# Regrouping the operand preparation of a decoder layer at the end of its output projection, its FFN gate product and its tail

## The chip, the cores and the metric

The kernel runs on one core of a Trainium2 chip. The core has a matrix engine (TensorE; PE in the profile, with PEld for its weight loads), a vector engine (VectorE, DVE), a scalar engine (ScalarE, ACT), GpSimd (POOL) and SyncE (SP), which only issues DMA transfers here. Each engine works through its own list of instructions in order, and a list waits where an operand is not there yet. The metric is device time in microseconds (us) for one execution; 1256.14 us is the median of three runs before the change.

## The reference

One decoder layer for 1024 prompt tokens and 8 sample tokens, model width 1024. A projection w_in feeds a sliding-window attention and a retention (a linear recurrence in chunks of 128 tokens); both results, side by side, go through w_out; then follow a layer norm with a modulated residual, a SwiGLU FFN of width 2816, and a second layer norm. The shift, scale and gate of each residual come from a small product of `c` with w_ada. Cut to what matters here:

```
def ada_mod(c, w_ada, b_ada):
    m = jax.nn.silu(c) @ w_ada + b_ada
    shift, scale, gate = jnp.split(m, 3, axis=-1)
    return shift[:, None, :], scale[:, None, :], gate[:, None, :]

def swiglu(h, w_up, w_down):
    g, u = jnp.split(h @ w_up, 2, axis=-1)
    return (jax.nn.silu(g) * u) @ w_down

def reference(...):
        mp, kp, vp, sp = mixer_prompt(yp * (1.0 + scp) + shp, ...)     # ends with concat([att, ret]) @ w_out
        ms, ks, vs, ss = mixer_sample(ys * (1.0 + scs) + shs, ...)
        yp = layer_norm(DEEPNORM_ALPHA * yp + (1.0 + gtp) * mp, ln1_w[l], ln1_b[l])
        ys = layer_norm(DEEPNORM_ALPHA * ys + (1.0 + gts) * ms, ln1_w[l], ln1_b[l])
        shp, scp, gtp = ada_mod(c_prompt, w_ada_ffn[l], b_ada_ffn[l])
        shs, scs, gts = ada_mod(c_sample, w_ada_ffn[l], b_ada_ffn[l])
        fp = swiglu(yp * (1.0 + scp) + shp, w_up[l], w_down[l])
        fs = swiglu(ys * (1.0 + scs) + shs, w_up[l], w_down[l])
        yp = layer_norm(DEEPNORM_ALPHA * yp + (1.0 + gtp) * fp, ln2_w[l], ln2_b[l])
```

## The kernel before

**Products.** Every large product is made of three matmuls (`mm3`, L215 to L217): the operands are float32, each is split into a high part (`h`, cast on ACT: L269 for w_in and w_out, L1347 in `split` for the FFN) and a low part (`l`, the difference on DVE: L281 and L1348), and h·h, l·h and h·l are added in PSUM. A weight's life is therefore: DMA into a `raw` (or `wr`) page, cast to `wh` on ACT, difference `wl` on DVE, then matmuls. One split of a 128x1024 page is one ACT and one DVE instruction. The FFN's products use a seven-product scheme, so its operands also need sums and differences of blocks (`up_sums`, L1366 to L1369, and `f_end` and `wd_sums`, L1480 to L1483 and L1513 to L1516) before they are split.

**What sets the order.** The program is written as Python generators. `Merge` runs a main generator (`in_group`, `out_proj`, `ffn`) and fills side streams in between: each stream yields the time that its piece is worth on PE and how long to wait, or a `need` that another stream marks as done. DVE, ACT and POOL run in the order that results from this; so the order in each engine's list is fixed when the program is built. Data pages come from one pool (`page`), so a load can be held by a page that is still in use.

**The stages in time.** The input projection (`pin`) with attention and the samples' retention `samp_ret` runs to 413 us; then `out_proj(0)`, which is the first 512 tokens, and `out_proj(1)`, together `pout`, with the retention chunks in between, to 544; then the FFN's first matrices (`up`, to 1027), then the down projection and the second layer norm (`dn`, to the end).

**Around the end of out_proj(1).** w_out has two column groups, `cg` 0 and 1, of four K-pairs `kp` each (`raw`, `wh`, `wl` of one unit). `w_get` fetches ahead by `depth`: how many units are loaded, cast and differenced in advance, [2, 1, 0] in half 0 and [4, 4, 3] in half 1. Column group 1 of half 1 is done tile by tile: all K for tile 0, then for tiles 1 to 3 (pout of four numbers on PE; m_0 to m_3 are the four pages of the mixed activations). The samples' share is `poutz`, gathered by `samp_sum` (L405 to L408: one copy and three adds into `otz`). Then, per tile, the gated residual (`otmp`, `xr`: L1117, L1118; `xrs` for the samples, L1126), the layer norm's statistics (L1217 to L1236) and the normalisation on ACT (L1238). The samples' `xrs` is transposed in `ln1_s` (`h2ps`, L1264), the prompt's `xr` in `h2_group(1)` (`h2p`, L1292). `h2_group` also makes the FFN's right-hand operands: `hb`, `ts`, `hs_0` to `hs_3`, `hc`. The weights of FFN matrix i are `wa`, `wb`, `wc`, `wd`, from two loads `wr`, prepared by `up_prep`.

**Other places the change touches.** `ada_gate_a` and `ada_gate_b` make the second gate (`which == 2`) from w_ada_ffn: loads `adr`, matmuls `adab` (L878) and `gsels` (L902), as a side stream during the input projection and `out_proj(0)`. In `samp_ret` (L949 on), the four state pages `st` and the four broadcasts `vb` are all loaded first. `f_end` and `wd_sums` for the last pair run right after the last `up`. `z_affine` (L1629) scales a 128x1024 page of the residual. `KM` is where the last column group of `dn` stops being done for all four tiles at a time: 11 K-steps, of which those from KM on are done tile by tile, three matmuls each.

Of the kernel before, what the change touches and what calls it, by code (L numbers as in the profile page):

```python
# [23 lines left out]
NP = NF // 2  # L24
# [13 lines left out]
KM = 4  # L38
# [139 lines left out]
def emit(ctx, tc, I, O):  # L178
# [644 lines left out]
    def ret_M(c):  # L823
# [4 lines left out]
        half, tl = c // 4, c % 4  # L828
        for j in range(2):
            mh, ml = mix_pages(half, 2 + j)  # L830
            oh = mh[:, 0:1024].rearrange("p (a c) -> p a c", a=2)[:, :, tl * 128:(tl + 1) * 128]
            ol = ml[:, 0:1024].rearrange("p (a c) -> p a c", a=2)[:, :, tl * 128:(tl + 1) * 128]
            for a in range(2):
                h = 2 * j + a
                src, g = b[:, h * 128:(h + 1) * 128], gnT[:, h:h + 1]
                A.mul(oh[:, a], src, g)
                V.scalar_tensor_tensor(out=ol[:, a], in0=src, scalar=g, in1=f(oh[:, a]), op0=ALU.mult,
                                       op1=ALU.subtract)
# [110 lines left out]
    def samp_ret():  # L949
# [5 lines left out]
        state_pg = []  # L955
        for i in range(4):
# [3 lines left out]
            state_pg.append(t)  # L960
# [3 lines left out]
        vb = []  # L964
        for i in range(4):
            t = page(f"vb{i}")
            SP.dma_start(out=t[:, 0:1024], in_=vd[2 * i:2 * i + 2, :].rearrange("(o b) e -> o (b e)", o=1)
                         .to_broadcast([128, 1024]))
            vb.append(t)
        yield 0, 4000, 3000  # L970
        b = bank("srt")
# [14 lines left out]
        for i in range(4):  # L986
            st = state_pg[i]
# [15 lines left out]
            yield 430, 0  # L1003
# [124 lines left out]
    def out_proj(half, with_s):  # L1128
        yield ("need", ("att", half))
        if half == 1:  # L1130
            depth[:] = [4, 4, 3]
        for cg in range(2):
# [334 lines left out]
    def f_end(P):  # L1467
# [16 lines left out]
        for p, ap in ((1, a11), (2, a12), (4, a22)):  # L1484
            d = drp.tile([128, 512], F32, name=f"fd{p}_{P}")
            G.dma_start(out=two(d) if p == 4 else d, in_=ap)  # L1486
            FD[p, P] = d
# [172 lines left out]
    def ffn():  # L1660
# [15 lines left out]
        f_end(NP - 1)  # L1676
        wd_sums(NP - 1)
# [135 lines left out]
    if True:  # L1813
# [20 lines left out]
        M.add([ada_gate_a(1), ada_gate_a(2)])  # L1834
# [61 lines left out]
```

## Time and profile before

| | value |
|---|---|
| time of the runs shown | 1257.42, 1256.14, 1255.63 us |
| the profiled execution: its time, its span | 1258.56 us, 1256.8 us |
| TensorE, busy | 1213.2 us, 97% of the span; 43.6 us not busy |
| VectorE, busy | 875.0 us, 70% |
| ScalarE, busy | 469.6 us, 37% |
| GpSimd, busy | 93.9 us, 7% |
| mean granted TensorE clock | 0.98 of full speed |
| w_up loads | 44 of 512 KB, 5.2 us each from issue to landing |

TensorE is the engine that is nearly always busy, so the profile is read for the places where it is not: what its instructions wait for (the view of waits), how busy each engine was in a stretch and at which clock (the view of windows), and the instructions one by one (the timeline). In a timeline row stand the start, the duration, the engine, the line and the operation, what goes in and out, how many alike were put together (x), and in brackets how long the engine had been idle before and which instruction ended that.

### The profile page before, as it was taken

What the parts mean: (1) busy time and instruction counts of PE and PEld (TensorE: products, weight loads), DVE (VectorE), ACT (ScalarE), POOL (GpSimd) and SP (SyncE); (2) the same over time, 40 slices, a digit from 0 to 9 for tenths busy, and PEclk for the clock granted to TensorE, in tenths of its full rate; (3) what the DMA queues carried; (4) which work ended last, traced back from release to release, by engine and by line L of the source; (5) the groups of instructions that cost most, each with busy time, mean ns of one, the idle gap of its engine ahead of it and who ended that gap; (6) DMA issues with size and microseconds to landing.
All of it is one profiled execution on the core that took longest, in us unless ns stands there. A gap on an engine that the chain in (4) does not pass through costs nothing.

```text
span 1256.8 us, 20184 instructions
## 1 busy us (share of the span) xinstructions
PE 1213.2 (97%) x7923; PEld 1023.8 (81%) x7923; DVE 875.0 (70%) x1749; ACT 469.6 (37%) x876; POOL 93.9 (7%) x130
## 2 busy tenths in 40 slices
PE   8999989999999999987999999999999999999996
PEld 5877756788877677677999999999999987888885
DVE  3456665787654687877767676667666769849697
ACT  2345543355543335545232322232223234434420
POOL 0000000001000002020110111011101110000011
PEclk8999999999999999997999999999999999999998
DMA  9732387242226432412443444344434499746631
GB/s 290 230 118 68 125 271 258 68 153 87 68 68 217 147 124 79 149 69 68 147 165 109 163 156 159 110 156 156 159 110 167 144 362 389 264 152 218 201 119 67
DMA packets 143999, 198.81 MB, mean 158 GB/s; under 512 B 8127, under 2 KB 85163, under 8 KB 143888
## 3 DMA queue, kind: packets, MB, share of 16 engines
q1 hardware_dynamic: 133376, 161.11, 39.6%
q0 software_dynamic: 10528, 36.42, 7.5%
q8 instruction: 62, 1.02, 0.3%
q14 instruction: 33, 0.27, 0.1%
HBM read 154.76 MB, written 43.77 MB: 158 GB/s over the span
## 4 chain that ended last, share of the span: by engine, by line
PE 54%; issue 29%; DVE 9%; POOL 4%; DMA 2%; ACT 1%; POOLq 0%; SPq 0%; DVEq 0%
PE pin L215 6%; PE pin L216 6%; PE pin L217 6%; PE dn L216 4%; PE dn L217 4%; PE dn L215 4%; PE up L215 2%; PE up L217 2%; PE up L216 2%; PE adab L878 2%; PE pout L215 1%; POOL fd L1486 1%; PE pv L671 1%; PE sps L628 1%; PE pout L216 1%
## 5 line engine op out<-in xcount | busy, mean ns | idle before, releaser
L215 PE MATMUL pin<-wh,hT 128*128 128x512 f32 (+1 forms) x320 | 129.6, 410 | 1.8 <-ACT qk L781 1.6
L216 PE MATMUL pin<-wl,hT 128*128 128x512 f32 (+1 forms) x320 | 124.8, 390 | 3.3 <-DVE wl L281 3.3
L217 PE MATMUL pin<-wh,hT 128*128 128x512 f32 (+1 forms) x320 | 124.3, 390 | 0.0
L215 PE MATMUL up<-hb,wa_h 128*128 128x256 f32 (+1 forms) x352 | 100.3, 286 | 6.9 <-ACT wa_h L1347 3.3
L216 PE MATMUL up<-hb,wa_h 128*128 128x256 f32 (+1 forms) x352 | 100.4, 285 | 0.4 <-DVE hb L1308 0.4
L217 PE MATMUL up<-hb,wa_l 128*128 128x256 f32 (+1 forms) x352 | 100.1, 285 | 0.2 <-DVE wa_l L1348 0.2
L215 PEld LDWEIGHTS pin<-wh,hT 128*128 128x128 f32 x320 | 61.1, 192 | 31.0 <-issue 13.9
L281 DVE TENSOR_TENSOR wl<-raw,wh 128x1024 fp32r<-128x1024 f32 (+1 forms) x62 | 73.1, 1183 | 7.3 <-ACT wh L269 3.6
L215 PEld LDWEIGHTS up<-hb,wa_h 128*128 128x128 f32 x352 | 67.3, 192 | 7.6 <-ACT wa_h L1347 3.5
L216 PEld LDWEIGHTS pin<-wl,hT 128*128 128x128 f32 x320 | 61.5, 192 | 14.4 <-DVE wl L281 3.4
L217 PEld LDWEIGHTS pin<-wh,hT 128*128 128x128 f32 x320 | 61.2, 191 | 14.0 <-issue 0.8
L1453 ACT ACTIVATE sg<-sg 128x256 f32<-128x256 f32 (+1 forms) x63 | 26.4, 420 | 115.3 <-DVE sg L1452 115.3
L216 PEld LDWEIGHTS up<-hb,wa_h 128*128 128x128 f32 x352 | 67.6, 192 | 0.6 <-DVE hb L1308 0.6
L217 PEld LDWEIGHTS up<-hb,wa_l 128*128 128x128 f32 x352 | 67.4, 192 | 0.4 <-DVE wa_l L1348 0.4
L269 ACT CAST wh<-raw 128x1024 fp32r<-128x1024 f32 (+1 forms) x62 | 62.9, 1020 | 6.8 <-DMA raw<-in_w_in 6.3
L1472 ACT COPY hTs<-sg 128x8 f32<-128x8 f32 x22 | 4.3, 198 | 138.9 <-DVE sg L1459 138.9
L1458 DVE TENSOR_TENSOR uc<-up,tp 128x256 f32<-128x256 f32 x66 | 28.2, 427 | 39.0 <-PE up L217 38.9
L1452 DVE TENSOR_TENSOR sg<-up,tp 128x256 f32<-128x256 f32 (+1 forms) x63 | 26.7, 423 | 38.2 <-PE up L217 38.2
L216 PE MATMUL pout<-wl,mh 128*128 128x512 f32 x128 | 50.8, 397 | 2.5 <-DVE wl L281 2.5
L215 PE MATMUL pout<-wh,mh 128*128 128x512 f32 x128 | 51.1, 408 | 0.0
L217 PE MATMUL pout<-wh,ml 128*128 128x512 f32 x128 | 51.0, 398 | 0.0
L215 PE MATMUL up<-hc,wc_h 128*128 128x256 f32 (+1 forms) x176 | 49.9, 284 | 0.0
(508 smaller groups left out, 3624.4 us busy)
## 6 DMA issues: line engine op xcount, KB each, us to landing
wr<-in_w_up SPq DMA_DIRECT2D x44, 512.0 KB, 5.2
raw<-in_w_in SPq DMA_DIRECT2D x38, 512.0 KB, 3.6
adr<-in_w_ada_ffn SPq DMA_DIRECT2D x24, 512.0 KB, 3.9
wd<-in_w_down SPq DMA_DIRECT2D x22, 512.0 KB, 5.2
dr<-fs SPq DMA_DIRECT2D x44, 256.0 KB, 2.8
dr<-ws SPq DMA_DIRECT2D x44, 256.0 KB, 3.7
fd<-sg POOLq DMA_DIRECT2D x33, 256.0 KB, 3.9
dr<-fd SPq DMA_DIRECT2D x33, 256.0 KB, 7.3
```

The lines of the kernel that those rows point to most:

```text
L215: PE.matmul(ps, lhsT=ah, rhs=bh, start=start, stop=False, skip_group_check=onto)
L216: PE.matmul(ps, lhsT=ah, rhs=bl, start=False, stop=False, skip_group_check=onto)
L217: PE.matmul(ps, lhsT=al, rhs=bh, start=False, stop=stop, skip_group_check=onto)
L269: A.copy(out=h[:, 0:n], in_=src[:, 0:n])
L281: V.tensor_sub(out=l[:, 0:n], in0=src[:, 0:n], in1=f(h[:, 0:n]))
L628: PE.matmul(bk[:, i1 * 256:i1 * 256 + n], lhsT=qT[b][:, h * 128:(h + 1) * 128], rhs=kv[:, k0 + off:k0 + 256], start=s == 0, stop=s == 1)
L671: PE.matmul(bk[64 * par:64 * par + 64, 0:256].rearrange("p (a c) -> p a c", a=2), lhsT=v, rhs=pv[:, kt, par::2, :], start=kt == k0, stop=k ...
L878: PE.matmul(b[32 * q:32 * q + 32, :], lhsT=cT[:, k2 * 4 + q, :], rhs=rr[q // 2][:, (q % 2) * 512:(q % 2) * 512 + 512], start=k2 == 0, stop ...
L1452: V.tensor_tensor(out=dst, in0=ps, in1=add, op=ALU.add)
L1453: A.activation(out=dst, in_=dst, func=AF.Silu)
L1458: V.tensor_tensor(out=t, in0=ps, in1=add, op=ALU.add)
L1486: G.dma_start(out=two(d) if p == 4 else d, in_=ap)
```

## The change

It makes eight edits.

- `samp_sum` copies 40 rows on ACT and adds twice on DVE instead of three times.
- `ret_M` issues four ACT multiplications, then four DVE instructions, instead of alternating.
- `samp_ret` loads `st` and `vb` in pairs: the first pair, the second after the ropes, the third and fourth when a pair has been used.
- The second gate (`ada_gate_a(2)`, `ada_gate_b(2)`) is a stream of its own behind the samples' normalised rows ("xns"), so it runs in `out_proj(1)` and the first FFN matrix.
- `depth` is [3, 2, 1] in half 0 and [3, 3, 2] in half 1.
- A new stream `up_first` prepares FFN matrix 0 as soon as the last of w_out has been fetched ("wload") and the sums and `wa` of matrix 1 once tile 7 is done; it ends with a one-column Silu on ACT. `ln1_s` waits for "outs", set right after `out_samp`, no longer for the whole of `out_proj(1)`.
- `f_end` for the last pair is stopped after its stores; its sums and `wd_sums` follow at steps 2 and 4 of the down projection, `samp_z` at 6, and the `z_affine` steps are spread by the list `ZAT`.
- `KM` is 3.

```diff
-KM = 4
+ZAT = [6, 8, 10, 12, 14, 16, 18, 20, 22, 24, 25, 26, 27, 28, 29, 30]
+KM = 3
...
     def samp_sum(dst, b, n):
-        A.copy(out=dst, in_=b[0:8, 0:n])
-        for g in range(1, 4):
-            V.tensor_tensor(out=dst, in0=dst, in1=b[32 * g:32 * g + 8, 0:n], op=ALU.add)
+        t = tmp512("ssum")
+        A.copy(out=t[0:40, 0:n], in_=b[0:40, 0:n])
+        V.tensor_tensor(out=t[0:40, 0:n], in0=t[0:40, 0:n], in1=b[64:104, 0:n], op=ALU.add)
+        V.tensor_tensor(out=dst, in0=t[0:8, 0:n], in1=t[32:40, 0:n], op=ALU.add)
...
+        for oh, ol, src, g in hs:
+            A.mul(oh, src, g)
+        for oh, ol, src, g in hs:
+            V.scalar_tensor_tensor(out=ol, in0=src, scalar=g, in1=f(oh), op0=ALU.mult, op1=ALU.subtract)
...
     def ada_gate_a(which):
+        if which == 2:
+            yield "need", "xns"
...
+        st_load(0)
         rr = page("rrs")
         ropefull(rr[0:8, 0:512], zqgs[:, 0:512], C("src")[0:8], C("srs")[0:8], 8)
         ropefull(rr[0:8, 512:1024], zkvs[:, 0:512], C("src")[32:40], C("srs")[32:40], 8)
...
         yield 0, 4000, 3000
+        st_load(1)
...
+            vb.pop(i)
+            if i < 2:
+                st_load(i + 2)
+            yield 430, 6000
...
     def out_proj(half, with_s):
         yield ("need", ("att", half))
-        if half == 1:
-            depth[:] = [4, 4, 3]
+        depth[:] = [3, 2, 1] if half == 0 else [3, 3, 2]
...
+                if half == 1 and cg == 1 and kp == 0:
+                    done.add("wload")
...
                 out_samp(cg, psz)
+                done.add("outs")
                 for t in range(4):
-                    if t == 1:
-                        up_prep(-AHEAD[1])
-                    if t == 2:
-                        up_prep(-AHEAD[0])
...
+    def up_first():
+        yield "need", "wload"
+        up_prep(-AHEAD[1])
+        yield 0, 4000
+        for n in (-3, -1, 1, 3):
+            up_prep(n)
+            yield 0, 0, 2500
+        yield "need", ("outt", 7)
+        done.add("first")
+        up_prep(0)
+        yield 0, 4000
+        up_prep(4)
+        t = small("silu", [128, 1])
+        A.activation(out=t, in_=identr[:, 0:1].bitcast(F32), func=AF.Silu)
+
     def ln1_s():
-        yield "need", ("out", 1)
+        yield "need", "outs"
...
-            if r[1] == 0 or "ahead" in done:
+            if r[1] == 0 or "ahead" in done or ("first" in done and r[0] <= 7):
...
-        f_end(NP - 1)
-        wd_sums(NP - 1)
+        fe = f_end(NP - 1)
+        next(fe)
+        for e in range(2):
+            r = (2 * (NP - 1) + e) * 128
+            WD[1 + e, NP - 1] = I["w_down"][r:r + 128, 0:512]
...
                 if n == 2:
+                    next(fe, None)
+                if n == 4:
+                    wd_sums(NP - 1)
+                if n == 6:
                     samp_z()
-                if 5 <= n < 21:
-                    z_affine((n - 5) // 2, (n - 5) % 2)
-                elif n == 21:
+                if n in ZAT:
+                    z_affine(ZAT.index(n) // 2, ZAT.index(n) % 2)
+                elif n == 23:
...
-        M.add([ada_gate_a(1), ada_gate_a(2)])
+        M.add([ada_gate_a(1)])
...
-        M.add([ada_gate_b(1), ada_gate_b(2)])
+        M.add([ada_gate_b(1)])
         M.run(out_proj(0, False), R3)
         M.add([ln1_tile(t) for t in range(4)] + [h2_group(0)], 2)
-        M.add([ln1_tile(t) for t in range(4, 8)] + [ln1_s(), h2_group(1)], 2)
+        M.add([up_first()])
+        M.add([ada_gate_a(2), ada_gate_b(2)])
+        M.add([ln1_s()])
+        M.add([ln1_tile(t) for t in range(4, 8)] + [h2_group(1)], 2)
```

How this moves instructions shows at three places. A row gives the line, the operation and out<-in; a number behind a name tells pages of one name apart, and the lines are some ten to thirty higher after the change.

**Place one: DVE in the input projection, around the samples' ropes (`rrs`, `rtmp`), the state updates (`st`) and a w_in difference.** Before:

```order
L719 TENSOR_TENSOR rrs<-rrs,rtmp 8x512 x2
L976 COPY qss<-srt 128x4x8
L977 TENSOR_SCALAR kss<-srt 128x4x8
L994 SCALAR_TENSOR_TENSOR st_1712<-vb_1731,kss,st_1712 128x128 x6
L281 TENSOR_TENSOR wl_1748<-raw_1594,wh_1707 128x1024
```

The same w_in difference, of raw_1594, in the changed kernel's DVE list:

```order
L718 TENSOR_TENSOR rrs<-zsr,cst 8x512
L282 TENSOR_TENSOR wl_1736<-raw_1594,wh_1707 128x1024
L721 TENSOR_TENSOR rrs<-rrs,rtmp 8x512
L718 TENSOR_TENSOR rrs<-zsr,cst 8x512
L721 TENSOR_TENSOR rrs<-rrs,rtmp 8x512
L984 COPY qss<-srt 128x4x8
```

The difference moved ahead of the last ropes and of six state updates.

**Place two: PE at the end of out_proj(1), column group 1.** The four tiles are pout_4998 to pout_5001 before and pout_4945 to pout_4948 after. Before, at the last tile's share of m_1 and what follows it:

```order
L217 MATMUL pout_5001<-wh_4758,ml_1_3257 128x512
L215 MATMUL pout_5001<-wh_4863,mh_2_4277 128x512
L1174 MATMUL poutz<-raw_4941,mixTs 32x512 x2
L216 MATMUL pout_4998<-wl_4945,mh_2_4277 128x512
L217 MATMUL pout_4998<-wh_4863,ml_2_4278 128x512
```

The changed kernel's PE list at the corresponding point, the end of the first three tiles' share of m_0:

```order
L217 MATMUL pout_4947<-wl_4812,mh_0_3133 128x512
L218 MATMUL pout_4947<-wh_4705,ml_0_3134 128x512
L216 MATMUL pout_4947<-wh_4810,mh_1_3187 128x512
L1186 MATMUL poutz<-raw_4888,mixTs 32x512
L217 MATMUL pout_4945<-wl_4892,mh_1_3187 128x512
L218 MATMUL pout_4945<-wh_4810,ml_1_3188 128x512
```

And where its third tile is complete:

```order
L217 MATMUL pout_4947<-wl_4965,mh_3_4236 128x512
L218 MATMUL pout_4947<-wh_4951,ml_3_4237 128x512
L1289 MATMUL h2ps<-cst,xrs 128x8 x8
L216 MATMUL pout_4948<-wh_4705,mh_0_3133 128x512
L217 MATMUL pout_4948<-wl_4812,mh_0_3133 128x512
L218 MATMUL pout_4948<-wh_4705,ml_0_3134 128x512
```

Before the change, the matmuls of m_0 and m_1 for all four tiles stand ahead of the first one that needs the third unit's difference (wl_4945, K-pair 2). After it, the matmuls of m_0 for three tiles stand ahead of the first one that needs the second unit's difference (wl_4892, K-pair 1), and the fourth tile stands behind the transposes of the samples' rows (h2ps), which in the kernel before come after all tiles.

**Place three: DVE at the same point, from the second half's first residuals on.** Before:

```order
L1118 SCALAR_TENSOR_TENSOR xr_3_4937<-xr_3_4937,otmp 128x512
L1126 SCALAR_TENSOR_TENSOR xrs<-xrs,otz 8x512
L281 TENSOR_TENSOR wl_4945<-raw_4861,wh_4863 128x1024
L281 TENSOR_TENSOR wl_5002<-raw_4941,wh_4943 128x1024
L408 TENSOR_TENSOR otz<-otz,poutz 8x512 x3
```

The changed kernel's DVE list, at the first of its differences of column group 1 that stands behind the residuals:

```order
L1137 SCALAR_TENSOR_TENSOR xrs<-xrs,otz 8x512
L1226 BN_STATS lst<-xrs 8x6
L1226 BN_STATS lst<-xr_0_4878 128x6
L282 TENSOR_TENSOR wl_4892<-raw_4808,wh_4810 128x1024
L1226 BN_STATS lst<-xr_1_4880 128x6
L282 TENSOR_TENSOR wl_4953<-raw_4888,wh_4890 128x1024
```

And, a little later, what stands between the samples' gated residual and its norm:

```order
L1137 SCALAR_TENSOR_TENSOR xrs<-xrs,otz 8x512
L1391 TENSOR_TENSOR sb_4985<-wr_1_4960 128x512
L1393 TENSOR_TENSOR sa_4984<-wr_0_4958,wr_1_4960 128x512
L1392 TENSOR_TENSOR sa_4984<-sb_4985,wr_0_4958 128x512
L1128 TENSOR_TENSOR otmp<-pout_4945,gate_4220 128x512
L1394 TENSOR_TENSOR sb_4985<-wr_0_4958,sa_4984 128x512
L1373 TENSOR_TENSOR wa_l<-wr_0_4958,wa_h 128x1024
L1373 TENSOR_TENSOR wb_l<-sa_4984,wb_h 128x1024
L1373 TENSOR_TENSOR wc_l<-sb_4985,wc_h 128x1024
L1414 TENSOR_TENSOR wd_5002<-wr_1_4960,wd_5002 128x512
```

So at this place DVE delivers the second unit's difference where it delivered the third's before, and all of FFN matrix 0's operands (sums sa, sb and differences wa_l, wb_l, wc_l, wd) are made in one piece behind the fourth unit.

More of the change, by code (lines that the diff above doesn't have):

```diff
@@ L828, in ret_M @@
         half, tl = c // 4, c % 4
+        hs = []
         for j in range(2):
@@ L834, in ret_M @@
                 h = 2 * j + a
[L835 to L838, printed above, removed]
+                hs.append((oh[:, a], ol[:, a], b[:, h * 128:(h + 1) * 128], gnT[:, h:h + 1]))
+        for oh, ol, src, g in hs:
+            A.mul(oh, src, g)
+        for oh, ol, src, g in hs:
+            V.scalar_tensor_tensor(out=ol, in0=src, scalar=g, in1=f(oh), op0=ALU.mult, op1=ALU.subtract)
     def ret_chunk(c):
@@ L954, in samp_ret, with st_load @@
         yield "need", ("zs", "rq")
-        state_pg = []
-        for i in range(4):
+        state_pg, vb = {}, {}
+        def st_load(i):
             t = page(f"st{i}")
@@ L959, in samp_ret @@
                          in_=I["state"][8 * i:8 * i + 8].rearrange("a d e -> d a e"))
-            state_pg.append(t)
+            state_pg[i] = t
+            t = page(f"vb{i}")
+            SP.dma_start(out=t[:, 0:1024], in_=vd[2 * i:2 * i + 2, :].rearrange("(o b) e -> o (b e)", o=1)
+                         .to_broadcast([128, 1024]))
+            vb[i] = t
+        st_load(0)
         rr = page("rrs")
@@ L963, in samp_ret @@
         ropefull(rr[0:8, 512:1024], zkvs[:, 0:512], C("src")[32:40], C("srs")[32:40], 8)
[L964 to L969, printed above, removed]
         yield 0, 4000, 3000
+        st_load(1)
         b = bank("srt")
@@ L986, in samp_ret @@
         for i in range(4):
-            st = state_pg[i]
+            st = state_pg.pop(i)
             s4 = st[:, 0:1024].rearrange("p (b h e) -> p b h e", b=2, h=4)
@@ L1002, in samp_ret @@
                         in_=st[:, 0:1024].rearrange("p (a e) -> p a e", a=8))
-            yield 430, 0
+            vb.pop(i)
+            if i < 2:
+                st_load(i + 2)
+            yield 430, 6000
         yield "need", ("zs", "rg")
@@ L1473, in f_end @@
                    in_=t[:, 512:NT].rearrange("p (b c) -> p b c", b=2)[:, :, 256:260])
-        sa, sb = page(f"fsa{P}"), page(f"fsb{P}")
         def two(ap):
             return ap.rearrange("p (b c) -> p b c", b=2)
+        for p, ap in ((1, a11), (2, a12), (4, a22)):
+            d = drp.tile([128, 512], F32, name=f"fd{p}_{P}")
+            G.dma_start(out=two(d) if p == 4 else d, in_=ap)
+            FD[p, P] = d
+        yield
+        sa, sb = page(f"fsa{P}"), page(f"fsb{P}")
         s2, s3, s1, s4 = sa[:, 0:512], sa[:, 512:1024], sb[:, 0:512], sb[:, 512:1024]
@@ L1483, in f_end @@
         V.tensor_sub(out=s4, in0=a12, in1=s2)
[L1484 to L1487, printed above, removed]
         for p2, t in (((6, 7), sa), ((5, 3), sb)):
@@ L1530, in emit @@
         n0 = 14 * (P + 1)
-        side.setdefault(n0, []).append((f_end, P))
+        side.setdefault(n0, []).append((lambda P: list(f_end(P)), P))
         side.setdefault(n0 + 1, []).append((wd_load, P))
```

## The prediction

> **What bounds the kernel now.** I read the busy times first, then what TensorE waits for, then the stretches in which it waits.
>
> ```profile
> span 1256.8 us, 20184 instructions
> PE 1213.2 (97%) x7923; PEld 1023.8 (81%) x7923; DVE 875.0 (70%) x1749; ACT 469.6 (37%) x876; POOL 93.9 (7%) x130
> ```
>
> TensorE is idle for 1256.8 - 1213.2 = 43.6 us; the other engines have room over the whole span. No matmul is removed, so the change can win only idle time, matmuls at a low clock, and the tail behind the last matmul. The view of waits (total us, times, longest) says where the idle time is:
>
> ```profile
> PE pin L216 <- DVE wl L281: 3.3, 1, 3.3
> ...
> PE pout L216 <- DVE wl L281: 2.5, 2, 1.2
> ...
> PE dn L216 <- DVE d_1l L1348: 1.6, 1, 1.6
> ...
> PE dn L216 <- DVE d_0l L1348: 1.1, 1, 1.1
> ...
> PE dn L216 <- DVE d_10l L1348: 0.4, 1, 0.4
> ```
>
> Nearly each row is one hole, and these wait for low parts (`wl`, `d_1l`) that DVE makes late. The windows show busy us of PE, PEld, DVE, ACT and POOL, then the granted clock:
>
> ```profile
> 180.00:190.00 10.00, 7.69 (x43) 5.34 (x44) 10.00 (x39) 0.84 (x2) 0.00 (x0) 0.83 0.79 259
> 390.00:450.00 60.00, 60.00 (x332) 41.73 (x328) 35.71 (x95) 19.57 (x43) 2.61 (x3) 0.97 0.48 167
> 450.00:460.00 10.00, 8.77 (x40) 6.54 (x40) 9.86 (x19) 6.85 (x16) 0.56 (x1) 1.00 0.50 133
> 580.00:590.00 10.00, 5.49 (x31) 4.42 (x31) 8.20 (x15) 5.24 (x10) 0.00 (x0) 0.82 0.39 107
> 590.00:600.00 10.00, 10.00 (x73) 10.00 (x73) 7.06 (x11) 4.22 (x6) 0.00 (x0) 0.84 0.21 61
> 515.90:590.00 74.10, 60.32 (x335) 48.81 (x335) 62.68 (x124) 34.65 (x50) 6.37 (x10) 0.91 0.28 90
> ```
>
> Behind holes the clock is 0.82 to 0.84 over 10 us, so a hole of about 3 us costs its length and (1 - 0.84) x 10 = 1.6 us more. From 390 to 450 TensorE is full, at 450 DVE is.
>
> **Input projection: -4.9 us.** The hole at 180:
>
> ```profile
> 176.34 1.28 DVE L719 TENSOR_TENSOR rrs<-rrs,rtmp 8x512 f32<-8x512 f32 x2
> 179.46 1.67 DVE L994 SCALAR_TENSOR_TENSOR st<-vb,kss,st 128x128 f32<-128x128 f32 x6
> 181.04 1.22 DVE L281 TENSOR_TENSOR wl<-raw,wh 128x1024 fp32r<-128x1024 f32 x1
> 182.31 0.50 PE L216 MATMUL pin<-wl,hT 128*128 128x512 f32 x1 [3.31 <-DVE wl L281]
> ```
>
> The difference waits behind ropes and six state updates. In the new order it stands ahead of the last ropes, near 176, some 5 us earlier, and TensorE needs it at 179. The hole goes (3.3) and the low clock after it (1.6): -4.9. What is late next is the second difference, which now stands behind 8 state updates (1.67 / 6 x 8 = 2.2 us) and has that slack. Bounds: -2 (the hole reappears there) to -5.
>
> By the Trainium skill (TensorE: Matmul & The Clock Gate, "What's actually happening") the half clock follows at least one idle window of about 3.4 us, of a window that runs freely. Here 3.31 us of idle time was enough. By the rule a hole just under the window may cost no clock, and this term would be -3.3; the row says -4.9, which I take.
>
> **The second gate: -5.9 us ahead of out_proj(1).**
>
> ```profile
> 417.38 1.06 PE L878 MATMUL adab<-adr,cT 128*32 128x512 f32 x8
> 441.53 1.03 PE L902 MATMUL gsels<-adg,cst 128*9 128x512 f32 x2
> ```
>
> Of the gate's products, four groups like the first (1.0 us from start to start) and two like the second (0.95) leave a stretch in which TensorE is full, by the window of 390 to 450: 4 x 1.0 + 2 x 0.95 = 5.9. With them go eight loads on SP and the evacuations on ACT. Later they fall into holes (below), where they cost nothing; if those holes close, the 5.9 come back there. At 450 DVE is 99% busy, so part of it may be given back by TensorE arriving early there: bounds 0 to -6. The other edits between 250 and 490 (the shorter `samp_sum`, four ACT multiplications first in `ret_M`, one unit more of fetching in half 0) touch holes of about 5 us and add none that I see: 0, bounds -2.5 to +2.5.
>
> **The end of out_proj(1): +5.5 us.** I count from U = 515.9, where column group 0 ends on TensorE.
>
> ```profile
> 516.00 1.06 PE L1174 MATMUL poutz<-raw,mixTs 128*32 128x512 f32 x8
> 522.71 0.40 PE L216 MATMUL pout<-wl,mh 128*128 128x512 f32 x1
> 522.95 0.40 PE L217 MATMUL pout<-wh,ml 128*128 128x512 f32 x1
> 525.74 1.21 DVE L1348 TENSOR_TENSOR hs_3l<-ts,hs_3h 128x1024 fp32r<-128x1024 f32 x1
> 527.58 0.69 DVE L1117 TENSOR_TENSOR otmp<-pout,gate 128x512 f32<-128x512 f32 x1
> 528.19 0.68 DVE L1217 BATCH_NORM_STATS2 lst<-xr 128x6 f32<-128x512 f32 x1
> 532.62 2.34 DVE L281 TENSOR_TENSOR wl<-raw,wh 128x1024 fp32r<-128x1024 f32 x2
> 533.88 0.50 PE L216 MATMUL pout<-wl,mh 128*128 128x512 f32 x1 [1.23 <-DVE wl L281]
> 543.94 0.40 PE L217 MATMUL pout<-wh,ml 128*128 128x512 f32 x1
> ```
>
> Before, the difference that stops TensorE is the third unit's, at 533.8, and the matmuls of two units in four tiles cover all but 1.23 us. The last pout starts at 543.94: T = U + 28.4.
>
> In the new order DVE does the same up to `hs_3l` (near 526.6), then eleven instructions of 0.61 from start to start (xr four times, otmp, ssum, otz twice, xrs, two statistics), then the difference: 526.6 + 6.7 + 1.2 = 534.5 = U + 18.6. But this is the second unit's, and ahead of it TensorE has only three tiles of the first: 21 matmuls x 0.23 (522.95 - 522.71) and nine `poutz` (the row above is four of them, 1.0 us), 7.1 us, so it runs dry at U + 7.5. **A hole of about 11 us.** Then the first three tiles, 51 matmuls, 12 us, bring it to U + 31.3.
>
> There the samples' transposes `h2ps` need the norm of `xrs`. On DVE it stands behind all of FFN matrix 0's preparation:
>
> ```profile
> 539.67 0.67 DVE L1366 TENSOR_TENSOR sb<-wr 128x512 f32<-128x512 f32 x1
> 543.53 1.25 ACT L1238 ACTIVATE xr<-xr,lrs 128x1024 f32<-128x1024 f32 x1 [9.23 <-DVE lrs L1236]
> 544.62 1.22 DVE L1348 TENSOR_TENSOR wa_l<-wr,wa_h 128x1024 fp32r<-128x1024 f32 x1
> ```
>
> The third and fourth differences and two `otz` and `xrs` end at U + 25; four sums and `wd` (5 x 0.61), three splits (3 x 1.2) and `otmp`, `xr`, statistics and small ones (4.5) give U + 36.6, the norm on ACT U + 38. A second hole of 6.5 us. Transposes, tile 3 (24 matmuls, 5.6 us) and a group of the gate follow: T = U + 45.4, or U + 47 with the low clock behind both holes. Thus T is 17 to 18.6 us later.
>
> What was to be won:
>
> ```profile
> 581.63 1.23 DVE L1348 TENSOR_TENSOR hs_3l<-ts,hs_3h 128x1040 fp32r<-128x1040 f32 x1
> 587.40 0.58 PE L215 MATMUL up<-hb,wa_h 128*128 128x256 f32 x1 [3.26 <-ACT wa_h L1347]
> ```
>
> Before, FFN matrix 1 starts at 587.40, 43.5 us behind T, and runs at half speed until 593; that costs about 2.6, so it effectively starts at 590.0 = U + 74.1. In the new order matrix 0's sums and splits (7 us of DVE) no longer lie between T and `hs_3l`, and matrix 1's sums and `wa` are made ahead of it. Walking the DVE list with the durations above, `hs_3l` ends 31.9 us behind T, and matrix 1 starts 1.3 later without its stall: U + 78.6 to U + 80.2. TensorE's work there, 169 FFN matmuls of 0.12, 32 transposes (3.7) and the rest of the gate (4.9), is 29 us and fits within 33. Difference to U + 74.1: +4.5 to +6; I take **+5.5**. Bounds: between U and 590, DVE is busy 62.7 of 74.1 us by the window, so no order wins more than 11.4; and +9 if the loads of w_out that now stand behind those of `xr` on SP come late as well.
>
> The same section of the Trainium skill speaks against this part: both holes are above its 3.4 us, so by it a cold stretch follows each for certain, which is the U + 80.2 case.
>
> The dummy Silu has no input that binds it to its place: its table load stands at the start of ACT's list, and the load ahead of the first real Silu is still there. It moves nothing: 0.
>
> **Down projection: -3.1 us.**
>
> ```profile
> 1027.40 0.69 DVE L1480 TENSOR_TENSOR fsb<-sg,sg 128x512 f32<-128x512 f32 x1
> 1029.41 1.04 ACT L1347 CAST d_1h<-dr 128x1024 fp32r<-128x1024 f32 x1
> 1032.34 1.22 DVE L1348 TENSOR_TENSOR d_1l<-dr,d_1h 128x1024 fp32r<-128x1024 f32 x1
> 1061.17 1.21 DVE L1629 TENSOR_TENSOR z<-z,ln_wb 128x1024 f32<-128x1024 f32 x1
> ```
>
> Eight sums of 0.61 from 1027.40 on stand ahead of `d_1l` and leave the place. Then ACT's cast bounds it: 1030.4 + 1.2 = 1031.6, and TensorE, which waited 1.6 us up to 1033.6, had matmuls until 1032.0, so that hole goes. By 1061 four of the z instructions (1.2 each) fewer have run on DVE, as `ZAT` spreads them; that covers the holes of 1.1 and 0.4 at `d_0l` and `d_10l`. 1.6 + 1.1 + 0.4 = 3.1. Bounds -1.5 (the eight sums, made some steps later, open the later holes again) to -3.4.
>
> **The tail: -1.5 us.**
>
> ```profile
> 1245.92 0.39 PE L217 MATMUL dn<-d_10h,d_10l 128*128 128x512 f32 x1
> 1242.49 0.69 DVE L1657 TENSOR_TENSOR zt<-dn,gate 128x512 f32<-128x512 f32 x1
> 1247.90 0.68 DVE L1657 TENSOR_TENSOR zt<-dn,gate 128x512 f32<-128x512 f32 x1
> ```
>
> DVE takes 5.4 us per tile (1242.49 to 1247.90), TensorE 21 x 0.232 = 4.9, so DVE falls behind; the last tile's norm starts at 1247.90, 1.6 us behind the end of the last matmul, 1246.31. With KM at 3 a tile takes 24 x 0.232 = 5.6 and DVE follows at once. Bounds 0 to -1.6.
>
> **Sum.** -4.9 - 5.9 + 5.5 - 3.1 - 1.5 = -9.9. Against the profiled execution, 1258.56 (span 1256.8 and 1.8 around it), that is 1248.7; it was 2.4 above the median 1256.14, so I forecast 1246.
>
> **Rivals.**
> - *The holes of out_proj(1) don't open* (the differences come earlier than my walk has them, since `hs` waits less): that term becomes -8 to -11, and the time 1230 to 1233. For it: DVE has 11.5 us of room there; against it: the order of its list is fixed, and eleven instructions stand ahead. 0.12.
> - *The gain ahead of out_proj(1) is eaten*: DVE is 99% busy at 450, so TensorE's 5.9 us become a wait there, and the low clock at 180 stays: -9.9 + 5.9 + 1.6 = -2.4 gives 1253.7. For it: that DVE row; against: from 390 to 450 DVE is busy for only 35.7 of 60 us, so it can work ahead. 0.20.
> - *out_proj(1) loses it all* (slower): one mechanism, the two late differences. If w_out's last two loads, now behind the four of `xr`, land late, the third and fourth difference open holes of their own, and T slips on. From +15.4 instead of +5.5 the sum is zero; at +19 the time is 1259.7. Against: the loads' pages come free with column group 0, 10 us ahead. 0.10.
> - *It doesn't do what it says:* of the preload of the table that holds; it is in the sum at 0.
>
> **How the numbers follow.** Forecast 0.58, the rivals as above. The range leaves out half of the first and nearly all of the slow case: 1232 to 1255. A measurement of this kernel can tell about 0.2% (2.5 us) from no change. Faster by more: the forecast, the first rival and half of the second, 0.80; within: the other half, 0.10; slower: 0.10.
>
> **What would show it.** No 3.3 us wait for `wl` in pin; gate products among `up`, none at 417; a wait of pout for `wl` of some 11 us and one of `h2ps` for ACT of some 6.5; no wait of `up` for `wa_h`; none of `dn` for `d_1l`; the last `zt` at once behind the last matmul. If the two long waits are absent, the first rival holds; if they are much longer, the third.

## The result and the profile after

The changed kernel takes 1262.95 us, the median of five runs (1262.29 to 1266.62), where the kernel before takes 1256.14 beside it: a ratio of 1.006, interval [1.0042, 1.0078]. It is slower by some 7 us, where 10 less were forecast, and lies outside the range. The profiled execution took 1266.6 us, with a span of 1264.8. Its page begins:

```profile
span 1264.8 us, 20175 instructions
PE 1217.7 (96%) x7923; PEld 1020.3 (81%) x7923; DVE 868.2 (69%) x1741; ACT 469.0 (37%) x879; POOL 93.2 (7%) x130
```

The span grew by 8.0 us, TensorE's idle time by only 3.5 (47.1 against 43.6): the other 4.5 is busy time, for the same 7923 matmuls. That is the first hint that this is not a story of waits alone. What TensorE waits for now (us in total, times, longest):

```profile
PE pout L217 <- DVE wl L282: 11.4, 3, 10.2
PE h2ps L1289 <- ACT xrs L1247: 5.8, 1, 5.8
PE up L216 <- DVE tp L1462: 4.4, 4, 2.0
PE rmt L829 <- DVE sm L755: 2.5, 2, 1.7
...
PE dn L217 <- DVE d_0l L1373: 1.1, 1, 1.1
PE dn L217 <- DVE d_8l L1373: 1.0, 1, 1.0
```

The waits of `up` for `wa_h` (3.3) and of `dn` for `d_1l` (1.6) are gone, that of `pin` for `wl` fell from 3.3 to 0.4, and two long ones are new, as forecast. In the timeline:

```profile
528.60 1.20 DVE L282 TENSOR_TENSOR wl<-raw,wh 128x1024 fp32r<-128x1024 f32 x1
529.85 0.80 PE L217 MATMUL pout<-wl,mh 128*128 128x512 f32 x1 [10.21 <-DVE wl L282]
...
532.71 1.93 PE L1186 MATMUL poutz<-raw,mixTs 128*32 128x512 f32 x6
...
535.30 0.69 DVE L409 TENSOR_TENSOR ssum<-ssum,poutz 40x512 f32<-40x512 f32 x1 [3.78 <-ACT ssum L408]
...
551.53 1.01 PE L1289 MATMUL h2ps<-cst,xrs 8*128 8x8 f32 x8 [5.81 <-ACT xrs L1247]
...
562.45 1.07 PE L882 MATMUL adab<-adr,cT 128*32 128x512 f32 x8
```

U (the second piece of `poutz`) now stands at 510.2. The late difference comes at U + 19.6 (forecast 18.6) and opens a hole of 10.21 us (forecast 11). `h2ps` starts at U + 41.3 (forecast 38): behind the hole `poutz` ran at half clock, 1.93 us, and DVE waited 3.78 for it. Its hole is 5.81 (forecast 6.5). The row of `adab` at 562 is the second gate's second group; its first stands at 555, behind both holes.

The windows below cut each profile at 30 us (behind the start, which the change leaves alone), at U, at the start of the first and at the end of the last `dn` matmul. The columns are the stretch, then busy us of PE, PEld, DVE, ACT and POOL, then the granted clock. The kernel before:

```profile
30.00:516.00 486.00, 477.64 (x2878) 362.27 (x2877) 316.50 (x846) 223.44 (x502) 20.49 (x28) 0.99 0.43 140
516.00:1027.30 511.30, 494.94 (x3939) 471.87 (x3938) 363.22 (x665) 157.43 (x276) 54.19 (x82) 0.98 0.44 145
1027.30:1246.30 219.00, 215.65 (x931) 173.08 (x930) 179.79 (x209) 81.86 (x85) 15.95 (x13) 1.00 0.61 214
```

The changed kernel, and below them the stretch from the last `pout` (T) to the start of FFN matrix 1, and two more:

```profile
30.00:510.20 480.20, 473.05 (x2846) 360.35 (x2844) 309.48 (x838) 219.07 (x500) 19.53 (x27) 0.99 0.42 134
510.20:1036.50 526.30, 503.19 (x3973) 470.89 (x3973) 363.36 (x664) 159.75 (x279) 53.99 (x83) 0.98 0.45 148
1036.50:1255.50 219.00, 216.60 (x934) 172.75 (x932) 180.93 (x211) 81.84 (x85) 16.86 (x14) 1.00 0.61 216
560.70:597.10 36.40, 33.55 (x231) 25.35 (x230) 24.41 (x53) 21.25 (x33) 1.51 (x3) 1.00 0.39 133
180.00:190.00 10.00, 10.00 (x65) 5.94 (x64) 6.41 (x27) 3.13 (x6) 0.00 (x0) 1.00 0.72 230
1050.00:1090.00 40.00, 37.99 (x160) 29.29 (x159) 39.94 (x39) 18.07 (x21) 2.74 (x4) 1.00 0.93 342
```

Each stretch is split three ways: *idle* is its length less PE's busy time; *low clock* is the busy time that a clock under 1 cost, the sum over windows of 2 us of busy time x (1 - granted clock); the rest is TensorE's *work*, what it would need at full clock without a wait. In us:

| | before | after | difference | forecast |
|---|---|---|---|---|
| 30 us to U: idle + low clock | 8.4 + 6.8 | 7.1 + 3.3 | -4.8 | -4.9 |
| U to the first `dn`: idle + low clock | 16.4 + 7.3 | 23.1 + 6.8 | +6.2 | +5.5 |
| work, 30 us to U | 470.9 | 469.8 | -1.1 | -5.9 |
| work, U to the first `dn` | 487.7 | 496.4 | +8.7 | 0 |
| first to last `dn` | 219.0 | 219.0 | 0.0 | -3.1 |
| behind the last `dn` | 10.5 | 9.4 | -1.1 | -1.5 |
| sum | | | +7.9 | -9.9 |

The two rows of idle time and low clock came out nearly as forecast, the first of them in part by luck (below). TensorE's work did not: -5.9 was expected, and it is +7.6.

### The profile page after: what moved, and what is told of

Read it like the earlier page. It is cut to its first block, busy times and chain, and to the rows that moved or that the text cites. A ratio compares the mean times of both kernels' runs of the same rounds, so it can differ in the third digit from the quotient of the medians.

```text
span 1264.8 us, 20175 instructions
## 1 busy us (share of the span) xinstructions
PE 1217.7 (96%) x7923; PEld 1020.3 (81%) x7923; DVE 868.2 (69%) x1741; ACT 469.0 (37%) x879; POOL 93.2 (7%) x130
## 4 chain that ended last, share of the span: by engine, by line
PE 42%; issue 28%; DVE 6%; POOL 4%; DMA 3%; ACT 1%; POOLq 0%; DVEq 0%; SPq 0%; ACTq 0%
PE dn L217 4%; PE dn L216 4%; PE dn L218 4%; PE pin L216 3%; PE pin L218 3%; PE pin L217 3%; PE up L216 2%; PE up L217 2%; PE up L218 2%; DMA dr<-fd 2%; PE pout L217 2%; PE pout L218 2%; PE pout L216 1%; POOL fd L1504 1%; POOL fs L1515 1%
## 5 line engine op out<-in xcount | busy, mean ns | idle before, releaser
L216 PE MATMUL pin<-wh,hT 128*128 128x512 f32 (+1 forms) x320 | 128.3, 405 | 0.8 <-ACT hT L340 0.8
L218 PE MATMUL pin<-wh,hT 128*128 128x512 f32 (+1 forms) x320 | 122.9, 384 | 0.0
L217 PE MATMUL up<-hb,wa_h 128*128 128x256 f32 (+1 forms) x352 | 99.1, 282 | 1.1 <-DVE hb L1333 1.1
L216 PE MATMUL up<-hb,wa_h 128*128 128x256 f32 (+1 forms) x352 | 99.0, 282 | 0.0
L217 PE MATMUL pout<-wl,mh 128*128 128x512 f32 x128 | 53.6, 420 | 11.4 <-DVE wl L282 11.4
```

What stands on the lines that cost most here:

```text
L216: PE.matmul(ps, lhsT=ah, rhs=bh, start=start, stop=False, skip_group_check=onto)
L217: PE.matmul(ps, lhsT=ah, rhs=bl, start=False, stop=False, skip_group_check=onto)
L218: PE.matmul(ps, lhsT=al, rhs=bh, start=False, stop=stop, skip_group_check=onto)
```

## The experiments

All in one table: the median of the runs, the ratio to the kernel before with its interval, the number of *packed pieces*, and the three parts of the stretch from 30 us to the first `dn`. A packed piece is an unbroken row, in PE's list, of the 32-column products `adab` and `poutz` (four matmuls make a whole group of `adab`); the number is counted in the programs.

| | time us | ratio | pieces | work | idle | low clock |
|---|---|---|---|---|---|---|
| before | 1256.14 | 1 | 24 | 958.6 | 24.8 | 14.1 |
| after | 1262.95 | 1.0060 [1.0042, 1.0078] | 30 | 966.2 | 30.2 | 10.1 |
| e1_depth | 1261.78 | 1.0043 [1.0024, 1.0062] | 29 | 964.7 | 27.4 | 12.1 |
| e2_first | 1261.76 | 1.0044 [1.0028, 1.0059] | 32 | 968.5 | 25.4 | 7.6 |
| e3_both | 1257.95 | 1.0020 [1.0004, 1.0036] | 31 | 965.7 | 23.5 | 9.0 |
| e4_qorder | 1256.50 | 1.0000 [0.9985, 1.0015] | 22 | 953.8 | 30.9 | 11.1 |
| e5_wlfirst | 1256.81 | 1.0012 [0.9998, 1.0027] | 31 | 966.4 | 22.9 | 6.9 |
| e6_gate_moved | 1249.83 | 0.9946 [0.9926, 0.9967] | 22 | 954.3 | 23.4 | 13.7 |
| e7_gate_back | 1257.38 | 1.0008 [0.9993, 1.0023] | 22 | 958.5 | 27.7 | 8.2 |
| e8_before_qorder | 1255.42 | 0.9996 [0.9973, 1.0019] | 22 | 956.0 | 21.9 | 10.0 |
| e9_lns_back | 1252.00 | 0.9969 [0.9956, 0.9982] | 22 | 955.7 | 23.9 | 11.8 |
| e10_first_kept | 1251.21 | 0.9963 [0.9949, 0.9976] | 23 | 955.8 | 23.9 | 10.2 |
| e11_sums_back | 1247.38, one run | | 22 | 956.7 | 23.5 | 6.7 |
| e12_samples_first | 1248.60 | 0.9945 [0.9926, 0.9964] | 23 | 956.3 | 23.6 | 8.4 |

Single executions of one kernel lie 3 to 6 us on either side of the median, mostly by stretches of low clock that come and go, so the last two columns of one profile are known to some 3 us only. The work is steadier: up to U, where the changed kernel, e1, e2, e3 and e5 have the same pieces, it is 469.3 to 469.9 in their profiles, while low clock is 3.3 to 6.8.

**Depth and stream.** One part undone at a time, then both.

```diff
-        depth[:] = [3, 2, 1] if half == 0 else [3, 3, 2]
+        depth[:] = [3, 2, 1] if half == 0 else [4, 4, 3]
```

> The changed kernel with the fetch-ahead of out_proj(1) set back to [4, 4, 3]; all else as changed. Theory A (two separate late deliveries): the 10.2 us wait of pout for wl goes with the low clock behind it, and the wait of h2ps for the samples' norm stays at about 6 us: some 11 us less than the changed kernel, 1252. Theory B (one chain on VectorE from the end of column group 0 to the samples' norm): the norm comes only earlier by what VectorE idles in that stretch (3.8 us behind poutz, and the second poutz pieces), so the wait moves from wl to h2ps, which grows to 11 to 13 us: some 4 us less, 1259.

1261.78 us. The waits for `wl` fell to 7.9 in total (longest 6.8) and did not go, as both theories had it; that of `h2ps` rose to 7.4, and T moved from U + 50.5 to U + 47.7 only. That is nearer to theory B: half of what is taken from the first hole stands in the second. Theory A (1252) falls, and the old depth alone does not close the first hole.

For the second, `up_first` goes, and `up_prep(-AHEAD[1])` and `up_prep(-AHEAD[0])` stand in the loop over the tiles again.

```diff
-        M.add([up_first()])
```

> The changed kernel without the new stream up_first: FFN matrix 0 prepared between the tiles as before the change; fetch-ahead stays [3, 3, 2]. Theory A: the 10.2 us wait of pout for wl stays, the 5.8 us wait of h2ps goes with its low clock: some 7 us less, 1256. Theory B: VectorE's preparation of matrix 0 (7 us) and the sums of matrix 1 only move behind tile 3 and lengthen the way from there to FFN matrix 1, whose wait for wa_h (3.3 us) comes back: within 2 us of the changed kernel, 1261 to 1265.

1261.76 us. The long wait for `wl` stays (10.2), and the waits of `up` for `wa_h` (2.8) and `wb_h` (1.4) come back, as theory B has it.

> The changed kernel with both undone: fetch-ahead [4, 4, 3] and no up_first. Theory A: both waits go, some 18 us less than the changed kernel, 1245. Theory B: the stretch from the end of column group 0 to FFN matrix 1 goes back to its length before the change (74 us against 87), some 13 us less, 1250.

1257.95 us: both theories were too good. Of its waits:

```profile
PE pout L217 <- DVE wl L282: 7.9, 3, 6.8
...
PE h2ps L1293 <- ACT xrs L1251: 1.3, 1, 1.3
```

With both parts undone the wait for `h2ps` is nearly gone, but a hole of 6.8 for `wl` stays, and the kernel is still not faster than before. Yet its idle time is 1.3 us below that of before and its low clock 5.1 below, while its work is 7.1 above. So the holes are not the whole cause: a part of it lies in TensorE's work.

**Packed pieces.** In the changed kernel many groups of `adab` are cut in two or three by other matmuls, since their four matmuls need two loads (`rr[0]` for q of 0 and 1, `rr[1]` for 2 and 3), of which the second comes later. With the order turned, the group waits for the later load and runs whole.

```diff
-            for q in range(4):
+            for q in (2, 3, 0, 1):
```

> The changed kernel with one edit in ada_block: the four matmuls of a group are issued in the order 2, 3, 0, 1, so that the first of them needs the later of the two loads; the list then has 16 whole groups of adab where the changed kernel has 24 pieces. Theory (a piece of the small products costs about 1.0 us on TensorE whether it holds one, two or four matmuls): five to eight pieces fewer ahead of the end of out_proj(1) and in FFN matrix 0, some 5 us less, 1258. Rival (a piece costs 0.25 us for each matmul in it): no change, 1262 to 1264.

1256.50 us: 6.4 us won against the changed kernel by the order of four matmuls, both holes as long as they were (10.2 and 6.1). What a piece costs is seen in PE's timeline. The changed kernel:

```profile
411.41 0.40 PE L218 MATMUL pout<-wh,ml 128*128 128x512 f32 x1
411.73 1.05 PE L882 MATMUL adab<-adr,cT 128*32 128x512 f32 x2
412.71 0.27 PE L1097 MATMUL spt<-cst,Ps 64*128 64x64 f32 x1
412.91 1.05 PE L882 MATMUL adab<-adr,cT 128*32 128x512 f32 x2
413.89 0.50 PE L216 MATMUL pout<-wh,mh 128*128 128x512 f32 x1
```

The same place with whole groups (e4_qorder):

```profile
408.56 0.40 PE L216 MATMUL pout<-wh,mh 128*128 128x512 f32 x1
408.88 1.06 PE L882 MATMUL adab<-adr,cT 128*32 128x512 f32 x8
409.88 0.50 PE L217 MATMUL pout<-wl,mh 128*128 128x512 f32 x1
410.22 0.39 PE L218 MATMUL pout<-wh,ml 128*128 128x512 f32 x1
```

The trace shows two records for each of these float32 matmuls. A piece of one matmul (x2) lasts 0.98 us from start to start, a piece of four (x8) 1.00. From 408.56 to 410.22 are 1.66 us, where two `pout` matmuls alone take 2 x 0.23 = 0.46: a piece costs 1.2 us. Over the fourteen rows of the table, a straight line through pieces and work rises by 1.23 us for a piece; six more pieces than before (five of `adab`, one of `poutz`) make 7.4, and the work rose by 7.6.

The same edit in the kernel before takes two pieces away:

> The kernel before with only the order 2, 3, 0, 1 in ada_block: 17 pieces of adab where it had 19. By the theory of pieces (1.0 us each): 2 us less, 1254 to 1255. By the rival (0.25 us for each matmul): no change, 1256 to 1257.

1255.42 us, interval [0.9973, 1.0019]. The work is 2.6 lower, but a gain of 2 us in the time can't be told from none here.

**The order around the two holes.** In `out_proj`, `w_get` is moved ahead of the loads of the residuals `xr` and `xrs`, so that the pages, and with them the order of DVE, put the second unit's difference eleven instructions earlier.

```diff
+                h, l, raw = w_get(("out", half, cg, kp))
                 if cg == 0 and kp == 3:
...
-                h, l, raw = w_get(("out", half, cg, kp))
```

> The changed kernel with the fetch of the last unit of column group 0 written ahead of the loads of xr and xrs (in both halves) instead of behind them. In VectorE's list the late difference then stands eleven instructions (6.7 us) earlier, right behind hs_3l; nothing else is taken away. Theory A (the late difference costs its wait): the wait of pout for wl falls from 10.2 to about 3.5 us and the time by some 6 us, 1257. Theory B (VectorE's whole chain to the samples' norm and on to FFN matrix 1 sets the end): the wait falls as much, the wait of h2ps grows by nearly as much, and the time falls by 0 to 2 us, 1261 to 1263.

1256.81 us, 6.1 less than the changed kernel: theory A, with 31 pieces still there. The longest wait for `wl` is 2.6 (5.5 in three waits), while that for `h2ps` is 6.4. So the first hole is worth about as much as the pieces. Next come whole groups and this edit, with depth and stream as before; the moved gate, `samp_sum`, the ropes and the end stay as changed.

> The changed kernel with whole adab groups (as e4), the fetch ahead of xr (as e5), fetch-ahead [4, 4, 3] and no up_first (as e3); the second gate still behind the samples' rows. From e3 (1258) by the pieces of adab (4 to 6 us) and an earlier third difference (2 to 4 us): 1249 to 1252.

1249.83 us, four runs: faster than both kernels, though TensorE stands idle for 7.9 us ahead of `h2ps`. Is that hole a loss?

```diff
-        yield "need", "outs"
+        yield "need", ("out", 1)
```

> As e6_gate_moved (1249.8 us), but the samples' transposes wait for the whole of out_proj(1) again, as before the change. In e6 TensorE stood 7.9 us ahead of them and ran eleven matmuls at half clock behind that. Theory A (a hole of TensorE there lies on the path): the hole goes, the last pout stands near U + 31 instead of U + 40.5, matrix 1 starts 6 to 9 us earlier, U + 66 to U + 69, and the time is 1241 to 1244. Theory B (the work of VectorE from U to hs_3l of matrix 1 sets the start of matrix 1, as in e7_gate_back, where there was no hole, wa_h was waited for 8.5 us and matrix 1 started at U + 73.7): matrix 1 starts at U + 73 to U + 74.5, the idle time only moves from h2ps to a wait of up for wa_h, and the time is 1248 to 1250.

```profile
PE up L216 <- ACT wa_h L1376: 7.3, 2, 5.2
...
PE up L218 <- DVE wa_l L1377: 2.0, 2, 1.6
```

1252.00 us, theory B in its steps, though 2 us above its range. The wait for `h2ps` is gone and waits for `wa_h` and `wa_l` stand in its place, as these rows of its waits show; matrix 1 starts at U + 75.3 instead of U + 74.8, and the idle time is 23.9 instead of 23.4. As long as DVE's work behind U sets the start of matrix 1, it does not matter where TensorE waits.

> The changed kernel with whole groups of the gate's products (as e4_qorder), w_out's fetch ahead of the residuals' loads (as e5_wlfirst) and the samples' transposes behind the whole of out_proj(1) (as e9_lns_back); depth [3, 3, 2] and the stream that prepares FFN matrix 0 in one piece stay as the change has them. Theory A (the two holes were the whole harm of the change here): neither hole, matrix 1 at U + 74 or earlier, 1247 to 1250 us. Theory B (depth and stream are late for their own sake: the third and fourth unit's differences and matrix 0's operands still stand behind the residuals): new waits of pout for wl or of up for wa_h of 4 us and more, matrix 1 at U + 78 or later, 1252 to 1255 us.

1251.21 us, between the theories: matrix 1 at U + 76.7, and no wait for `wl` above 1.1. Depth [3, 3, 2] and the stream do no harm of their own beyond what can be measured, once the difference comes early and the samples late.

```diff
+        M.add([ln1_s()])
         M.add([up_first()])
         M.add([ada_gate_a(2), ada_gate_b(2)])
-        M.add([ln1_s()])
```

> The changed kernel with whole groups of the gate's products (as e4_qorder), w_out's fetch ahead of the residuals' loads (as e5_wlfirst), and the samples' norm ahead of the stream that prepares FFN matrix 0, which otherwise stays, as do depth [3, 3, 2] and the mark outs. It tests an account that the runs so far suggest: matrix 1 starts at the later of two times, U + 75 (VectorE's own work behind U) and T + 35 (what stands behind the last tile, T being the last pout), so that T counts only beyond U + 40. Theory A (this account): the wait of h2ps for ACT shrinks to 4 us or less, T comes at U + 39 to U + 43 and matrix 1 at U + 75 to U + 78, and the time is 1249 to 1252 us. Theory B (preparing matrix 0 early is late for matrix 1 by itself, whatever T is): T as in A but matrix 1 at U + 81 or later, as in e5_wlfirst (U + 82.1), and 1254 to 1257 us.

1248.60 us, ratio 0.9945 [0.9926, 0.9964]: the changed kernel with three edits of order, faster than both kernels. The time is theory A's, but its steps are not: `h2ps` still waits 7.3 us, T is at U + 46.7, and matrix 1 at U + 81.0, where theory B had it. T + 34.3 fits the account, and up to the first `dn` it took 514.8 us from U, 516.0 in e6. From matrix 1 to `dn` are 433.8 us here and 441.2 there, for the same work (432.1 and 432.6): all of the gate stands ahead of matrix 1 in both, but in e6 matrix 1 starts behind a wait of 2.7 us and at a low clock. The first 20 us of matrix 1, in e6 and below it here:

```profile
580.20:600.20 20.00, 19.08 (x138) 18.72 (x139) 14.49 (x24) 5.56 (x8) 0.00 (x0) 0.85 0.24 66
584.50:604.50 20.00, 20.00 (x170) 20.00 (x169) 15.86 (x31) 5.47 (x11) 0.81 (x3) 1.00 0.36 104
```

So the start of matrix 1 alone is a bad measure: an early start that meets waits and low clock wins little.

**The moved gate.** The second gate at its old place, ahead of out_proj(1), without its wait for "xns", and everything else as in e9_lns_back:

```diff
-        M.add([ada_gate_a(1)])
+        M.add([ada_gate_a(1), ada_gate_a(2)])
```

> As e6, with the second gate back in the input projection and out_proj(0), and ln1_s behind the whole of out_proj(1) again. What remains of the change is samp_ret, samp_sum, ret_M, the fetch-ahead in half 0, and the down projection's edits. If moving the gate behind the samples' rows is worth its 5.9 us of TensorE, this is some 5 us slower than e6, 1254 to 1257; if the gate's products come back in FFN matrix 0, where TensorE runs beside a VectorE that has no room, it is the same or faster, 1247 to 1251.

1257.38 us, ratio 1.0008 [0.9993, 1.0023], against 0.9969 [0.9956, 0.9982] with the gate moved (e9_lns_back): moving it is worth 0.4%, some 5 us, with whole groups and without the first hole. U stands at 510.6 with the gate ahead of it and at 503.2 without; from U to the first `dn` are 513.9 and 518.2 us, so even here more than half came back. This kernel still has the edits of the input projection, of the down projection and of the tail, and it is not faster than the kernel before: what the table of the stretches credits to them (-4.8, 0.0, -1.1) does not show in its time. Behind U it idles for 20.2 us against 16.4 before; the smaller edits were not undone one at a time.

**The deferred sums.** As e6_gate_moved, with the last pair's sums back at the projection's end.

```diff
-                if n == 2:
-                    next(fe, None)
-                if n == 4:
-                    wd_sums(NP - 1)
```

> As e6_gate_moved, but the last pair's sums and the two weight sums run at once behind the last up again, as before the change; the spread z steps and KM at 3 stay. Read in the stretch from the first to the last dn matmul, which took 219.0 us before the change and 218.6 to 219.1 in all kernels with it. Theory A (the sums are only moved: VectorE's work by the middle of the down projection stays the same, so what is won at d_1l is lost at later differences): the wait for d_1l of 1.6 us comes back, the waits for d_8l and d_0l (1.0 and 1.1) shrink or go, the stretch stays within 218.5 to 219.5. Theory B (the deferral wins its 1.6 us and something else in the stretch loses as much): the wait for d_1l comes back, d_8l and d_0l stay, and the stretch takes 220 to 221 us.

Its waits of `dn` are, to within a tenth, those of the kernel before:

```profile
PE dn L217 <- DVE d_1l L1377: 1.6, 1, 1.6
PE dn L217 <- DVE d_0l L1377: 1.1, 1, 1.1
PE dn L217 <- DVE d_10l L1377: 0.4, 1, 0.4
PE dn L217 <- DVE d_9l L1377: 0.2, 1, 0.2
```

The stretch takes 219.3 us, 218.6 with the sums deferred. Theory A in its main point: the deferral takes away 1.6, 0.4 and 0.2 and opens 1.0 at `d_8l`; the wait for `d_0l` does not care. The 0.7 us between the two stretches are one profile against one.

## Why the prediction was wrong

**Input projection (-4.9): right for the hole, luck in the sum.** The window at 180 has PE 10.00 busy at clock 1.00 instead of 7.69 at 0.83, so the wait of 3.3 us and the low clock behind it are gone. But of the 3.3 us, 2 came back in small new holes, and low clock up to U fell by 3.5, of which the hole explains some 1.7. The rest is the chance of one execution: in e8_before_qorder `pin` still waits 3.3 us for `wl` at this place, yet its idle time and low clock up to U are 8.3 + 2.6 only. Against that execution the changed kernel's 7.1 + 3.3 are a gain of 0.5, not 4.8.

**The second gate (-5.9): the step that failed.** The products did leave the place (none at 417), but "Later they fall into holes (below), where they cost nothing" was wrong, and so was counting them as four groups of one piece. First, the new order also cut groups that stayed: ahead of U the work fell by 1.1 only. Second, behind U they were paid in full, +8.7: one group of the gate is in three pieces there, and `poutz` in one piece more. The forecast had 29 us of TensorE's work in the 33 us from T to matrix 1, where DVE was to set the pace. The window from 560.7 to 597.1 has TensorE busy for 33.55 of 36.40 us and DVE for 24.41: TensorE had become the bound there (from 581.7 to matrix 1 it waits for nothing), since DVE had made matrix 0's operands ahead of T. The holes end at 529.9 and 551.5, and the products stand from 555 on, most of them behind T; none is inside a hole. With all of the work counted to it, this term came out at +7.6, a miss of 13.5 of the 17.8 us between forecast and result. e4_qorder shows the part of the pieces: with eight pieces fewer, 6.4 us less time by the medians, and 12.4 us less work by the profiles (that of the changed kernel is 3.6 us above its median), where eight pieces at 1.2 make 9.6.

**The end of out_proj(1) (+5.5): right in mechanism and nearly in size.** Both holes opened as walked, 10.21 and 5.81 us. With low clock the stretch lost 6.2. TensorE ran dry at U + 9.4 instead of U + 7.5, as the nine `poutz` matmuls there came in four pieces: the same miscount as that of the gate. The second hole ended 3 us late: DVE waited 3.78 us for the `poutz` behind the first hole, a wait that the walk had left out. By an estimate from the rows, 2.4 of it is the half clock (matmuls 0.43 us apart instead of 0.23, and 1.93 for `poutz` instead of 1.0). Half clock came behind both holes, up to 535.6 and 556.7, as the prediction's U + 80.2 case has it; one execution does not show that it is certain. T before was U + 28.0 (543.94 - 515.9), not 28.4, but the sum does not use it.

**Down projection (-3.1): wrong, 0.0.** The waits for `d_1l` and `d_10l` went, as forecast, but from 1050 to 1090 DVE is busy for 39.94 of 40 us, and `d_8l` opened a hole of 1.0, which e11_sums_back does not have: the sums were moved into a stretch that has no room. The bound of -1.5 named this. `ZAT` did not cover `d_0l`: its wait is 1.1 with the sums at either place. Idle time fell by 0.9, and TensorE's busy time rose by 0.95: it is 216.1 to 216.8 us in all kernels with the new tail and `KM` at 3, and 215.6 and 215.8 in the two with `KM` at 4 (before, e8). Why, no run settled.

**The tail (-1.5): right, -1.1.** The last `zt` starts 0.5 us behind the last matmul instead of 1.6:

```profile
1255.96 0.68 DVE L1682 TENSOR_TENSOR zt<-dn,gate 128x512 f32<-128x512 f32 x1
```

**The rivals.** The first failed, since both holes opened. The slow one had the right sign and the wrong mechanism: of the 11.4 us of waits for `wl` the first hole is 10.2 and the rest stands ahead of U, so the third and fourth difference opened nothing. The gain ahead of out_proj(1) was eaten indeed, but by TensorE's own pieces rather than by a wait on DVE at 450.

## What to carry to other kernels

Work that is moved to where an engine has holes is free only if it stands in the list inside those holes; ask which engine is the bound in the stretch where the moved instructions really land. When a change reorders a list, count the pieces into which packed products fall, not only their matmuls, and compare an engine's work at full clock (length less idle time less low clock) between the two profiles before looking at waits. A hole that only moves along a chain set by another engine costs nothing that these runs can tell.

## What the runs showed of the hardware

A piece of the 32-column products takes TensorE the same time with one matmul as with four (0.98 and 1.00 us), and 1.2 us in all. By the Trainium skill (TensorE: Matmul & The Clock Gate, "Measured speedup vs the span model") a pack takes one matmul's time and about 4 ns for each further one: the trace agrees for columns, with 0.02 us for three further ones. The same skill (TensorEngine Tiling (Array Packing), "Key Properties") says that changing the tiling mode drains TensorE, which would fit the 0.2 us beyond; no run here measured that alone.

TensorE can lose its clock while it is busy. In e4_qorder 16 small matmuls with 9 columns each (32 records) run without a gap from 218.3 to 221.9:

```profile
218.28 3.63 PE L940 MATMUL adft<-cst,adf 128*128 128x9 f32 x32
...
223.04 0.51 PE L217 MATMUL pin<-wl,hT 128*128 128x512 f32 x1
223.35 0.63 PE L218 MATMUL pin<-wh,hT 128*128 128x512 f32 x1
```

Behind them the windows of the same kernel show no idle time, and half clock:

```profile
222.00:224.00 2.00, 2.00 (x11) 1.17 (x14) 1.89 (x7) 0.72 (x1) 0.00 (x0) 0.79 0.00 0
224.00:226.00 2.00, 2.00 (x9) 0.34 (x10) 0.72 (x3) 0.00 (x0) 0.00 (x0) 0.50 0.00 0
226.00:228.00 2.00, 2.00 (x13) 1.75 (x12) 1.16 (x2) 0.32 (x1) 0.00 (x0) 0.86 0.00 0
```

The loss is 2 x (0.21 + 0.50 + 0.14) = 1.7 us. In the changed kernel the same matmuls (223.0 to 226.6) cost no clock. The Trainium skill (TensorE: Matmul & The Clock Gate, "What's actually happening") has the clock set by how busy TensorE is, in a window of about 3.4 us that runs freely. That a stretch of small matmuls counts only where it covers such a window would fit both cases; no run here tested it. One such episode costs 1.7 us. Executions with a lower mean clock are the longer ones (of e7_gate_back, 1252.98 us at 0.985 and 1259.15 at 0.980), so such episodes explain a good part of the spread.
